# A hybrid decoder layer: the first norm's inverse root, GpSimd's early scaling, the first weight loads and two heads' key copies rearranged

## The chip, the core and the metric

The kernel runs on one core of a Trainium2 chip. The core has TensorE for matmuls (PE in the profile), VectorE (DVE), ScalarE (ACT), GpSimd (POOL) and SyncE (SP), which issues most DMAs. Each engine takes its instructions in order and waits on semaphores for the others. The metric is the device time of one execution in microseconds (us). A lower time is better.

## The reference

One decoder layer for a sequence of 1024 tokens and 1024 features, all in float32:

```python
u = rms_norm(x, g1);  aq, ak, av, hq, hf, hi, hg = split(u @ w_in)
attn = rms_norm(dilated_attention(aq, ak, av), g_a)      # 8 heads of 64
rec  = rms_norm(hgrn2(hq, hf, hi), g_h) * silu(hg)       # 4 heads of 128
h = x + concat(attn, rec) @ w_out
u = rms_norm(h, g2);  gate, val = split(u @ w_up)
h = h + (gelu(causal_conv3(gate)) * val) @ w_down
out = rms_norm(h, gf)      # rms_norm(x, g) = x * rsqrt(mean(x*x) + 1e-6) * g
```

## The kernel before

Data lie with features on the 128 partitions and tokens along a row. The sequence is worked in two halves of 512 tokens, called 0 and 1. Each float32 product is made from three matmuls on a pair of a rounded high part and a low remainder (`hi*hi`, `hi*lo`, `lo*hi`), so each operand is split first: a high copy and a subtraction. A `Ring` does it for the weights: it loads 128x512 pieces into `raww` by a DMA on SP's queue (L66), makes `whi` on ScalarE (L86) and `wlo` on VectorE or GpSimd (L88). Two pieces of head 1 go to buffers called `thw` and `tlw`.

The part that the change touches is the start, the first 62 us or so.

- **Load and split of x.** Eight chunks per half come in by SP (L389). `scale_x` makes `uhi` on ScalarE (L396) and `ulo` on VectorE (L397). `square_x` and `sum_x` collect the sum of squares. All these, and the first weights, are pinned in the order in which the code is written.
- **First products.** TensorE first runs some products of ones (`busy`, L380), then the combined query and key projections of heads 0 and 1, chunk by chunk (L459 to L462): two chunks of head 0, then the first two of head 1, and from there in turns.
- **The norm of x.** `rms1(hf)` sums the squares over partitions with a matmul and calls `rstd` twice: for `R1` (128x512) and for `R1T` (128x4, the same values with tokens on partitions). `rstd` takes Ln and Exp on ScalarE and sharpens the result with one Newton step of four VectorE operations (L319 to L322). `R1` scales `x` of a head (L548), `R1T` scales the values `v` (L566, L567).
- **A head's queries and keys** (`evac` in `qk_half`): `x = ps * R1` on VectorE, `qs` and one key copy on ScalarE (L549, L550), the second key copy, the low part of `qs` and `kl` on VectorE (L551, L552, L554). The zero halves of the two `kl` buffers are set by GpSimd at the start (L535).
- **Scores and values.** `score_steps(h, j)` makes the scores S (L584, L585) and P of two blocks of 128 queries: VectorE adds the mask and takes the row extreme (L587, and a 128x1 combination L591 where a row has two pieces), ScalarE takes Exp (L592), VectorE the reciprocal (L593), GpSimd multiplies (L596). `value_steps` transposes P on TensorE (L611 to L618) and multiplies by the values. The scores of (head 0, pair j+1) run beside the value steps of pair j, with other products filled in between.

TensorE's order is written out by hand. Where instructions of the other engines aren't pinned, a scheduler places them by its own costs. So a changed operation can shift the places of its neighbours. One DMA of `vec`, a table of gains and biases, is issued by ScalarE at the very start (L216). GpSimd then multiplies some of its columns by constants (L448), which are used much later.

Of the kernel before, what the change touches and what calls it, by code (L numbers as in the profile page):

```python
# [13 lines left out]
AF = mybir.ActivationFunctionType  # L14
ALU = mybir.AluOpType
PSUM = bass.MemoryType.PSUM

P = 128
SEQ = 1024
DM = 1024  # L20
# [6 lines left out]
EPS = 1e-6  # L27
# [6 lines left out]
V_AG = 8  # L34
V_HG = 12
V_LB = 16
V_G2 = 24
V_CW = 32
V_CB = V_CW + 3 * NFF
V_GF = V_CB + NFF  # L40
# [3 lines left out]
def f32(ap):  # L44
    return ap.bitcast(F32)


class Ring:


    def __init__(self, nc, pool, plan, tag="w", raws=5, depth=5, low=None):
        self.nc, self.pool, self.tag = nc, pool, tag
        self.RAWS, self.DEPTH, self.low = raws, depth, low or nc.gpsimd
        self.plan, self.at, self.live, self.n = list(plan), 0, {}, 0
        self.raws = 0
        self.aside = {}
        self.on_vector = ()
        self.order = self.pin = lambda ins: ins
        self.high = nc.scalar.copy

    def raw(self, src=None):
        t = self.pool.tile([P, H2], F32, tag=f"raw{self.tag}", name=f"raw{self.tag}{self.raws}", bufs=self.RAWS)
        self.raws += 1
        if src is not None:
            t = t[:, : src.shape[-1]]
            self.order(self.nc.sync.dma_start(t, src))  # L66
        return t

    def fill(self, count=99):
        while count and self.at < len(self.plan):  # L70
            key, src = self.plan[self.at]
            other = key in self.aside
            if (other and self.aside[key] is None) or (not other and self.n == self.DEPTH):
                return
            count -= 1
            i = self.at
            self.at += 1
            raw = src(self) if callable(src) else self.raw(src)
            w = raw.shape[-1]
            if other:  # L80
                hi, lo = self.aside[key](i)
            else:
                self.n += 1
                hi = self.pool.tile([P, H2], F32R, tag=f"{self.tag}hi", name=f"{self.tag}hi{i}", bufs=self.DEPTH)
                lo = self.pool.tile([P, H2], F32R, tag=f"{self.tag}lo", name=f"{self.tag}lo{i}", bufs=self.DEPTH)
            self.pin(self.high(hi[:, :w], raw))  # L86
            low = self.nc.vector if key in self.on_vector or key[0] in self.on_vector else self.low
            self.pin(low.tensor_sub(lo[:, :w], raw, f32(hi[:, :w])))  # L88
            self.live[key] = (hi, lo)
# [113 lines left out]
def hybrid_kernel(ctx: ExitStack, tc: tile.TileContext, xT, w_qk, w_tok, w_hg, w_out, w_up,  # L203
                  w_down, vecs, amask, hmask, out):
    nc = tc.nc
    PE, DVE, ACT, POOL = nc.tensor, nc.vector, nc.scalar, nc.gpsimd
    ctx.enter_context(tc.manual_schedule(engines={mybir.EngineType.PE}))

    def pool(name, side, **kw):
        return tc.tile_pool(name=name, bufs=1, side=side, reuse_waits="tile", **kw)  # L210
# [4 lines left out]
    vec = cpool.tile([P, V_N], F32, name="vec")  # L215
# [5 lines left out]
    lb = cpool.tile([P, 96], F32, name="lb")  # L221
    epool = ctx.enter_context(pool("eps", "right"))
    eps_ = epool.tile([P, 120], F32, name="eps")
    epst = eps_[:, 0:1]
    rv_cm = pool("rv", "right")
    rv = rv_cm.__enter__()
    ident = rv.tile([P, P], F32, name="ident")
    R1T = rv.tile([P, P], F32, name="R1T")
    DVE.memset(ones, 1.0)
    DVE.memset(eps_, EPS)  # L230
    make_identity(nc, ident)

    halves = [slice(0, H2), slice(H2, SEQ)]
# [75 lines left out]
    ring = Ring(nc, ringp, plan)  # L309
# [2 lines left out]
    def col(j):  # L312
        return vec[:, j : j + 1]

    def rstd(y, ms, t, ss, inv):

        ACT.activation(t, ss, AF.Ln, bias=epst, scale=inv)
        ACT.activation(y, t, AF.Exp, scale=-0.5)
        DVE.tensor_scalar(ms, ss, inv, EPS, op0=ALU.mult, op1=ALU.add)  # L319
        DVE.tensor_mul(t, y, y)  # L320
        DVE.scalar_tensor_tensor(ms, t, -0.5, ms, op0=ALU.mult, op1=ALU.mult)
        DVE.scalar_tensor_tensor(y, ms, 1.5, y, op0=ALU.add, op1=ALU.mult)  # L322
        return y

    def rstd_part(y, t, ss, inv):
# [20 lines left out]
    def rtile(name, dt=F32):  # L346
        return rv.tile([P, H2], dt, tag="r", name=name, bufs=8)
# [8 lines left out]
    R1 = up_.tile([P, SEQ], F32, name="R1")  # L356
# [4 lines left out]
    def bank(tag, name):  # L361
        return ps1.tile([P, H2], F32, tag=tag, name=name, bufs=2)
# [22 lines left out]
    pin = tc.keep_in_program_order  # L385
    xts = {hf: vtile([P, NCT, H2], F32, f"xt{hf}") for hf in range(2)}

    def load_x(hf, c):
        pin(nc.sync.dma_start(xts[hf][:, c], xT[c, :, halves[hf]]))  # L389
# [3 lines left out]
    def scale_x(hf, c):  # L393
        t = halves[hf]
        x = xts[hf][:, c]
        pin(ACT.mul(uhi[:, c, t], x, col(V_G1 + c)))  # L396
        pin(DVE.scalar_tensor_tensor(ulo[:, c, t], x, col(V_G1 + c), f32(uhi[:, c, t]), op0=ALU.mult, op1=ALU.subtract))  # L397
# [12 lines left out]
    def rms1(hf):  # L410
        ss = bank("t", f"ss{hf}")
        PE.matmul(ss, ones, sums[hf], start=True, stop=True)
        st = bank("t", f"sst{hf}")
        for i in range(4):
            PE.matmul(st[:, i : i + 1], sums[hf][:, i * P : (i + 1) * P], ones[:, 0:1], start=True, stop=True)
        rstd(R1[:, halves[hf]], rtile(f"ms{hf}"), rtile(f"rt{hf}"), ss, 1.0 / DM)
        tm = rv.tile([P, 64], F32, name=f"rst{hf}")
        rstd(R1T[:, 4 * hf : 4 * hf + 4], tm[:, 0:4], tm[:, 4:8], st[:, 0:4], 1.0 / DM)


    ring.order = ring.pin = pin
    load_x(0, 0)
    ring.high = DVE.tensor_copy
    ring.fill(1)
# [2 lines left out]
    load_x(0, 1)  # L427
    scale_x(0, 1)
    ring.fill(1)
    for c in (2, 3):  # L430
        load_x(0, c)
        scale_x(0, c)
# [11 lines left out]
            square_x(0, 4 + c, pin)  # L444
            sum_x(0, 4 + c, pin)
    ring.order = ring.pin = lambda ins: ins
    for v, n, inv in ((V_AG, 4, 1.0 / 512), (V_HG, 4, 1.0 / P), (V_G2, 8, 1.0 / DM), (V_GF, 8, 1.0 / DM)):
        POOL.tensor_scalar(vec[:, v : v + n], vec[:, v : v + n], -0.5 * inv, 0.0, op0=ALU.mult, op1=ALU.add)  # L448


    def dense(key, hf, evac, last, tag="mm"):

        t = halves[hf]
        ps = bank(tag, f"p{key}{hf}".translate({ord(x): "_" for x in "(', )"}))
        for c in range(NCT):
            hi, lo = ring.get((key, c // 4))
            s = slice((c % 4) * P, (c % 4 + 1) * P)
            b = between.get((key, hf, c), (0, 0))
            PE.matmul(ps, hi[:, s], uhi[:, c, t], start=(c == 0), stop=False)  # L459
            busy(b[0])  # L460
            PE.matmul(ps, hi[:, s], ulo[:, c, t], start=False, stop=False)
            PE.matmul(ps, lo[:, s], uhi[:, c, t], start=False, stop=(c == NCT - 1))  # L462
            busy(b[1])
            if last and c % 4 == 3:
                ring.done((key, c // 4))
            yield 0.65
        evac(ps)
# [60 lines left out]
    if True:  # L528
# [4 lines left out]
        for i in range(NQ):  # L533
            kl = at.tile([P, SEQ], F32R, name=f"kl{i}")
            POOL.memset(f32(kl[64:128]), 0.0)  # L535
            kls.append(kl)
        qk = {}

        def qk_half(h, hf, last, tag="mm"):
            t = halves[hf]  # L540

            def evac(ps):
                if hf == 0:
                    qk[h] = (at.tile([P, SEQ], F32R, tag="qs", name=f"qs{h}", bufs=NQ),
                             at.tile([P, SEQ], F32R, tag="kh", name=f"kh{h}", bufs=NQ), kls[h % NQ])
                qs, kh, kl = qk[h]
                x = at.tile([P, H2], F32, tag="x", name=f"x{h}_{hf}")
                DVE.tensor_mul(x, ps, R1[:, t])  # L548
                ACT.mul(qs[0:64, t], x[0:64], DH ** -0.5)  # L549
                ACT.copy(kh[64:128, t], x[64:128])  # L550
                DVE.tensor_copy(kh[0:64, t], x[64:128])  # L551
                DVE.scalar_tensor_tensor(qs[64:128, t], x[0:64], DH ** -0.5, f32(qs[0:64, t]),  # L552
                                         op0=ALU.mult, op1=ALU.subtract)
                DVE.tensor_sub(kl[0:64, t], x[64:128], f32(kh[64:128, t]))  # L554
            return dense(("qk", h), hf, evac, last, tag)
# [115 lines left out]
        for c in range(NCT):  # L671
            for g in pairs[1]:
                next(g)
            if c == 2:
                rms1(0)
                for g in pairs[0]:
                    next(g, None)
                ring.fill()
# [10 lines left out]
        fill.add(v0[3])  # L689
        fill.run()  # L690
        rms1(1)
        for c in range(4):
            for hf in range(2):
# [62 lines left out]
    with pool("hg", "right") as hg:  # L756
# [75 lines left out]
        tm = hg.tile([P, NG], F32, name="lb_m")  # L832
# [406 lines left out]
    with pool("ps2", "left", space=PSUM) as ps2:  # L1239
# [159 lines left out]
        for x, y in STAGES:  # L1399
# [27 lines left out]
            for d in range(KS):  # L1427
                src = ps[d]
# [3 lines left out]
                elif x == "s2":  # L1432
                    DVE.tensor_add(X[d], ps[d], X[d])
                    src = X[d]
# [83 lines left out]
```

## Time and profile before

| what | us |
|---|---|
| median of 3 runs | 1211.65 |
| lowest and highest | 1210.78 and 1213.84 |
| the profiled execution's own time | 1211.85 |
| its span in the trace | 1209.9 |
| PE busy in the span | 1193.9 (99%) |
| DVE busy | 951.6 (79%) |
| ACT busy | 627.2 (52%) |
| POOL busy | 299.2 (25%) |

The span runs from the first to the last traced instruction. 1.95 us of the execution's time lie around it. Busy shares are averages over stages with different limits. What a change at one place is worth is read at that place: which wait ends last there.

### The profile page before, as it was taken

The numbers are of one execution on the slowest core, as the hardware profiler recorded it, in microseconds if no ns is written. First come the engines' busy times: TensorE is split into PE (matmuls) and PEld (weight loads), VectorE is DVE, ScalarE is ACT, GpSimd is POOL, SyncE is SP. The second block draws the span as 40 slices with busy tenths as digits, with TensorE's granted clock in tenths as the row PEclk, the third lists the DMA queues.
The fourth block names the chain that finished last, engine by engine and source line by source line (L and its number), as shares of the span: only waits on it lengthen the run. The fifth ranks groups of instructions, "written<-read, shape, count | busy, mean of one in ns | idle before, by whom it ended". The sixth has DMA issues, their size and how long they took to land.

```text
span 1209.9 us, 17468 instructions
## 1 busy us (share of the span) xinstructions
PE 1193.9 (99%) x6014; PEld 1006.8 (83%) x6014; DVE 951.6 (79%) x1792; ACT 627.2 (52%) x1205; POOL 299.2 (25%) x278
## 2 busy tenths in 40 slices
PE   9999999999999999999999999999999999999996
PEld 7988888888888888888888888888888888888886
DVE  8867776666778776484999889898798878957986
ACT  8566667667656655454643343433434444444553
POOL 1254446545001014413221322312223100000000
PEclk9999999999999999999999999999999999999998
DMA  7021112123111123442023322333223267435532
GB/s 257 25 70 54 53 53 80 61 62 115 53 36 53 53 62 113 124 137 96 35 71 114 109 86 101 122 114 109 83 97 122 96 209 252 150 99 156 171 100 92
DMA packets 71817, 122.39 MB, mean 101 GB/s; under 512 B 7344, under 2 KB 17840, under 8 KB 71728
## 3 DMA queue, kind: packets, MB, share of 16 engines
q1 hardware_dynamic: 60928, 101.80, 26.8%
q10 hardware_dynamic: 10800, 19.47, 4.2%
q8 instruction: 47, 0.77, 0.3%
q14 instruction: 42, 0.34, 0.1%
HBM read 97.65 MB, written 23.59 MB: 100 GB/s over the span
## 4 chain that ended last, share of the span: by engine, by line
PE 93%; issue 2%; DVE 2%; ACT 1%; POOL 0%; DMA 0%; SPq 0%; DVEq 0%; ACTq 0%; POOLq 0%
PE p L1125 10%; PE p L1123 10%; PE p L1124 10%; PE ds L1418 3%; PE ds L1417 3%; PE ds L1416 3%; PE po L1027 2%; PE po L1029 2%; PE po L1028 2%; PE da L1418 2%; PE da L1417 2%; PE da L1416 2%; PE S L584 1%; PE piv L513 1%; PE S L585 1%
## 5 line engine op out<-in xcount | busy, mean ns | idle before, releaser
L88 POOL TENSOR_TENSOR wlo<-raww,whi 128x512 fp32r<-128x512 f32 x141 | 207.5, 1482 | 383.5 <-ACT whi L86 274.1
L86 ACT CAST whi<-raww 128x512 fp32r<-128x512 f32 x276 | 168.3, 618 | 190.6 <-DVE raww L120 64.8
L88 DVE TENSOR_TENSOR wlo<-raww,whi 128x512 fp32r<-128x512 f32 x136 | 97.4, 716 | 22.6 <-ACT whi L86 22.5
L86 ACT CAST whi<-r 128x512 fp32r<-128x512 f32 x70 | 43.6, 622 | 83.6 <-PE ds L1417 51.4
L596 POOL TENSOR_SCALAR P<-P,st 128x512 f32<-128x512 f32 (+2 forms) x96 | 56.3, 596 | 110.8 <-DVE st L593 62.2
L587 DVE CUSTOM_DVE_ANT_0 P<-S,mask 128x512 f32<-128x512 f32 (+2 forms) x96 | 52.1, 553 | 29.9 <-PE S L585 29.0
L592 ACT ACTIVATE P<-P,st 128x128 f32<-128x128 f32 (+3 forms) x64 | 49.7, 776 | 32.9 <-DVE st L587 16.6
L623 DVE TENSOR_TENSOR tl<-T,th 128x512 fp32r<-128x512 f32 (+1 forms) x80 | 50.7, 634 | 16.6 <-ACT th L622 15.6
L88 DVE TENSOR_TENSOR wlo<-r,whi 128x512 fp32r<-128x512 f32 x70 | 47.9, 686 | 20.2 <-ACT whi L86 20.1
L1418 PE MATMUL ds<-fhi,wlo 128*128 128x512 f32 x160 | 62.3, 389 | 0.0
L1417 PE MATMUL ds<-flo,whi 128*128 128x512 f32 x160 | 62.3, 389 | 0.0
L1416 PE MATMUL ds<-fhi,whi 128*128 128x512 f32 x160 | 62.2, 389 | 0.0
L1123 PE MATMUL p<-b1h,whi 128*128 128x512 f32 x160 | 62.2, 389 | 0.0
L1124 PE MATMUL p<-b1l,whi 128*128 128x512 f32 x160 | 62.2, 389 | 0.0
L1125 PE MATMUL p<-b1h,wlo 128*128 128x512 f32 x160 | 62.2, 389 | 0.0
L1145 DVE SCALAR_TENSOR_TENSOR cv<-g,vec,cv 128x511 f32<-128x511 f32 (+2 forms) x92 | 56.1, 615 | 4.7 <-ACT cv L1142 3.7
L1390 POOL TENSOR_TENSOR facc<-facc,sqf 128x256 f32<-128x256 f32 x4 | 2.9, 732 | 223.1 <-ACT sqf L1389 223.1
L1152 ACT ACTIVATE cv<-cv 128x512 f32<-128x512 f32 x44 | 27.8, 633 | 55.6 <-DVE cv L1145 55.5
L622 ACT CAST th<-T 128x512 fp32r<-128x512 f32 (+1 forms) x80 | 42.9, 536 | 23.5 <-PE T L615 20.9
L86 ACT CAST fhi<-rawf 128x512 fp32r<-128x512 f32 x70 | 43.1, 616 | 15.2 <-DMA rawf<-spT 6.5
L88 DVE TENSOR_TENSOR flo<-rawf,fhi 128x512 fp32r<-128x512 f32 x70 | 47.9, 684 | 4.0 <-ACT fhi L86 4.0
L1416 PE MATMUL da<-fhi,whi 128*128 128x512 f32 x120 | 46.7, 389 | 0.0
(670 smaller groups left out, 3833.5 us busy)
## 6 DMA issues: line engine op xcount, KB each, us to landing
raww<-in_w_up_dram SPq DMA_DIRECT2D x88, 256.0 KB, 3.1
raww<-in_w_tok_dram SPq DMA_DIRECT2D x52, 256.0 KB, 2.6
rawf<-spT SPq DMA_DIRECT2D x40, 256.0 KB, 2.7
r<-in_w_down_dram SPq DMA_DIRECT2D x40, 256.0 KB, 3.4
raww<-in_w_hg_dram SPq DMA_DIRECT2D x32, 256.0 KB, 2.6
raww<-in_w_out_dram SPq DMA_DIRECT2D x32, 256.0 KB, 2.6
spB<-a ACTq DMA_DIRECT2D x30, 256.0 KB, 2.3
spT<-t ACTq DMA_DIRECT2D x30, 256.0 KB, 2.0
```

What stands on the lines that cost most here:

```text
L86: self.pin(self.high(hi[:, :w], raw))
L88: self.pin(low.tensor_sub(lo[:, :w], raw, f32(hi[:, :w])))
L587: DVE.tensor_tensor_reduce(Pt[:, k0 : k0 + w], S[:, :w], mask[:, m : m + w], -1.0, BIG * 3, op0=ALU.add, op1=ALU.min, accum_out=st[:, k0 / ...
L596: POOL.tensor_scalar(e, e, st[:, 3:4], 1.0, op0=ALU.mult, op1=ALU.mult)
L623: DVE.tensor_sub(tl[:, :n], T[:, :n], f32(th[:, :n]))
L1123: PE.matmul(ps, hi[:, s], bhi, start=(start and n == 0), stop=False)
L1124: PE.matmul(ps, hi[:, s], blo, start=False, stop=False)
L1125: PE.matmul(ps, lo[:, s], bhi, start=False, stop=(stop and n == len(rhs) - 1))
L1145: DVE.scalar_tensor_tensor(dst, x, col(V_CW + j * NFF + f), dst, op0=ALU.mult, op1=ALU.add)
L1416: PE.matmul(ps[d], hi[:, s], ahi, start=(k == 0), stop=False)
L1417: PE.matmul(ps[d], hi[:, s], alo, start=False, stop=False)
L1418: PE.matmul(ps[d], lo[:, s], ahi, start=False, stop=(k == NPAIR - 1))
```

## The change

Five edits, all in the first stage.

1. `rstd` no longer makes the mean `ms` first. Exp's result is squared on ScalarE, VectorE multiplies it by the sum plus a constant (one operation), ScalarE applies `1.5 - 0.5*inv*t` (Identity with a bias from a column of `eps`), and VectorE multiplies by Exp's result. So each call has two VectorE operations where there were four, and two more on ScalarE. `rstd` is called four times: `R1` and `R1T`, each for both halves.
2. The constant tile `eps` gets 1.5 in its upper columns, by a second memset.
3. GpSimd's scaling of `vec` moves behind the memsets of `kl`, and is pinned there.
4. The DMAs of the first two weight pieces go out on ScalarE's queue instead of SP's.
5. For heads 0 and 1 the second key copy is made by ScalarE, not by VectorE (four instructions, one per head and half).

```diff
--- before.py
+++ after.py
@@ -57,13 +57,14 @@
         self.on_vector = ()
         self.order = self.pin = lambda ins: ins
         self.high = nc.scalar.copy
+        self.queue = nc.sync
 
     def raw(self, src=None):
         t = self.pool.tile([P, H2], F32, tag=f"raw{self.tag}", name=f"raw{self.tag}{self.raws}", bufs=self.RAWS)
         self.raws += 1
         if src is not None:
             t = t[:, : src.shape[-1]]
-            self.order(self.nc.sync.dma_start(t, src))
+            self.order(self.queue.dma_start(t, src))
         return t
 
     def fill(self, count=99):
@@ -221,13 +222,14 @@
     lb = cpool.tile([P, 96], F32, name="lb")
     epool = ctx.enter_context(pool("eps", "right"))
     eps_ = epool.tile([P, 120], F32, name="eps")
-    epst = eps_[:, 0:1]
+    epst, onehalf = eps_[:, 0:1], eps_[:, 64:65]
     rv_cm = pool("rv", "right")
     rv = rv_cm.__enter__()
     ident = rv.tile([P, P], F32, name="ident")
     R1T = rv.tile([P, P], F32, name="R1T")
     DVE.memset(ones, 1.0)
-    DVE.memset(eps_, EPS)
+    DVE.memset(eps_[:, 0:64], EPS)
+    DVE.memset(eps_[:, 64:120], 1.5)
     make_identity(nc, ident)
 
     halves = [slice(0, H2), slice(H2, SEQ)]
@@ -312,14 +314,14 @@
     def col(j):
         return vec[:, j : j + 1]
 
-    def rstd(y, ms, t, ss, inv):
+    def rstd(y, t, ss, inv):
 
         ACT.activation(t, ss, AF.Ln, bias=epst, scale=inv)
         ACT.activation(y, t, AF.Exp, scale=-0.5)
-        DVE.tensor_scalar(ms, ss, inv, EPS, op0=ALU.mult, op1=ALU.add)
-        DVE.tensor_mul(t, y, y)
-        DVE.scalar_tensor_tensor(ms, t, -0.5, ms, op0=ALU.mult, op1=ALU.mult)
-        DVE.scalar_tensor_tensor(y, ms, 1.5, y, op0=ALU.add, op1=ALU.mult)
+        ACT.activation(t, y, AF.Square)
+        DVE.scalar_tensor_tensor(t, ss, EPS / inv, t, op0=ALU.add, op1=ALU.mult)
+        ACT.activation(t, t, AF.Identity, bias=onehalf, scale=-0.5 * inv)
+        DVE.tensor_mul(y, t, y)
         return y
 
     def rstd_part(y, t, ss, inv):
@@ -413,12 +415,13 @@
         st = bank("t", f"sst{hf}")
         for i in range(4):
             PE.matmul(st[:, i : i + 1], sums[hf][:, i * P : (i + 1) * P], ones[:, 0:1], start=True, stop=True)
-        rstd(R1[:, halves[hf]], rtile(f"ms{hf}"), rtile(f"rt{hf}"), ss, 1.0 / DM)
+        rstd(R1[:, halves[hf]], rtile(f"rt{hf}"), ss, 1.0 / DM)
         tm = rv.tile([P, 64], F32, name=f"rst{hf}")
-        rstd(R1T[:, 4 * hf : 4 * hf + 4], tm[:, 0:4], tm[:, 4:8], st[:, 0:4], 1.0 / DM)
+        rstd(R1T[:, 4 * hf : 4 * hf + 4], tm[:, 0:4], st[:, 0:4], 1.0 / DM)
 
 
     ring.order = ring.pin = pin
+    ring.queue = nc.scalar
     load_x(0, 0)
     ring.high = DVE.tensor_copy
     ring.fill(1)
@@ -427,6 +430,7 @@
     load_x(0, 1)
     scale_x(0, 1)
     ring.fill(1)
+    ring.queue = nc.sync
     for c in (2, 3):
         load_x(0, c)
         scale_x(0, c)
@@ -444,8 +448,6 @@
             square_x(0, 4 + c, pin)
             sum_x(0, 4 + c, pin)
     ring.order = ring.pin = lambda ins: ins
-    for v, n, inv in ((V_AG, 4, 1.0 / 512), (V_HG, 4, 1.0 / P), (V_G2, 8, 1.0 / DM), (V_GF, 8, 1.0 / DM)):
-        POOL.tensor_scalar(vec[:, v : v + n], vec[:, v : v + n], -0.5 * inv, 0.0, op0=ALU.mult, op1=ALU.add)
 
 
     def dense(key, hf, evac, last, tag="mm"):
@@ -534,6 +536,8 @@
             kl = at.tile([P, SEQ], F32R, name=f"kl{i}")
             POOL.memset(f32(kl[64:128]), 0.0)
             kls.append(kl)
+        for v, n, inv in ((V_AG, 4, 1.0 / 512), (V_HG, 4, 1.0 / P), (V_G2, 8, 1.0 / DM), (V_GF, 8, 1.0 / DM)):
+            pin(POOL.tensor_scalar(vec[:, v : v + n], vec[:, v : v + n], -0.5 * inv, 0.0, op0=ALU.mult, op1=ALU.add))
         qk = {}
 
         def qk_half(h, hf, last, tag="mm"):
@@ -548,7 +552,7 @@
                 DVE.tensor_mul(x, ps, R1[:, t])
                 ACT.mul(qs[0:64, t], x[0:64], DH ** -0.5)
                 ACT.copy(kh[64:128, t], x[64:128])
-                DVE.tensor_copy(kh[0:64, t], x[64:128])
+                (ACT.copy if h < 2 else DVE.tensor_copy)(kh[0:64, t], x[64:128])
                 DVE.scalar_tensor_tensor(qs[64:128, t], x[0:64], DH ** -0.5, f32(qs[0:64, t]),
                                          op0=ALU.mult, op1=ALU.subtract)
                 DVE.tensor_sub(kl[0:64, t], x[64:128], f32(kh[64:128, t]))
```

The scheduler moves other instructions with these. At the start of ScalarE's queue, `raww0` and `raww1` are the first pieces of the weights of heads 0 and 1, and `uhi` the first chunks of x. Before:

```order
L216 DMA vec_63<-in_vecs_dram 128x128
L217 ACT_TABLE_LOAD
L396 ACTIVATE uhi_86<-xt0_104,vec_63 128x512 x2
L86 CAST thw1_120<-raww1_118 128x512
L396 ACTIVATE uhi_86<-xt0_104,vec_63 128x512 x2
L86 CAST whi2_132<-raww2_130 128x512
L86 CAST thw3_138<-raww3_136 128x512
```

After:

```order
L217 DMA vec_63<-in_vecs_dram 128x128
L218 ACT_TABLE_LOAD
L67 DMA raww0_108<-in_w_qk_dram 128x512
L398 ACTIVATE uhi_87<-xt0_105,vec_63 128x512 x2
L67 DMA raww1_119<-in_w_qk_dram 128x512
L87 CAST thw1_121<-raww1_119 128x512
L398 ACTIVATE uhi_87<-xt0_105,vec_63 128x512 x2
L87 CAST whi2_133<-raww2_131 128x512
L87 CAST thw3_139<-raww3_137 128x512
```

The second weight load now stands behind two activations that wait for chunks of x, and `thw1`, which needs that load, right behind it. On SP's queue at the start, before (`mask` is the attention mask, 512 KB, `xt` the chunks of x, `raww4` the first value weights):

```order
L389 DMA xt0_104<-in_xT_dram 128x512
L66 DMA raww0_107<-in_w_qk_dram 128x512
L389 DMA xt0_104<-in_xT_dram 128x512
L66 DMA raww1_118<-in_w_qk_dram 128x512
L389 DMA xt0_104<-in_xT_dram 128x512 x2
L66 DMA raww2_130<-in_w_qk_dram 128x512
L66 DMA raww3_136<-in_w_qk_dram 128x512
L389 DMA xt0_104<-in_xT_dram 128x512 x4
L389 DMA xt1_105<-in_xT_dram 128x512 x8
L530 DMA mask_205<-in_amask_dram 128x1024
L66 DMA raww4_328<-in_w_tok_dram 128x512
```

After:

```order
L391 DMA xt0_105<-in_xT_dram 128x512 x4
L532 DMA mask_202<-in_amask_dram 128x1024
L67 DMA raww2_131<-in_w_qk_dram 128x512
L67 DMA raww3_137<-in_w_qk_dram 128x512
L391 DMA xt0_105<-in_xT_dram 128x512 x4
L391 DMA xt1_106<-in_xT_dram 128x512 x8
L67 DMA raww4_328<-in_w_tok_dram 128x512
```

Besides the two weight loads that left, the mask has moved ahead of the second weight pieces and of chunks 4 to 7 of x. On VectorE around the norm of half 1 (`rt1`, `rst1` and `ms1` are its temporaries, `x0_1` is head 0's projection of half 1, `P0_2` and `P0_3` are blocks of its scores), before:

```order
L322 SCALAR_TENSOR_TENSOR R1_88<-ms1_545,R1_88 128x512
L322 SCALAR_TENSOR_TENSOR R1T_76<-rst1_553,R1T_76 128x4
L587 ISA P0_2_595,st0_2_596<-S0_2_0_597,mask_205 128x384
L587 ISA st0_2_596 128x1
L548 TENSOR_TENSOR x0_1_632<-p__qk___0_1_268,R1_88 128x512
L567 SCALAR_TENSOR_TENSOR v0_436<-pV0_4_568,R1T_76,v0_436 128x4x64
L593 RECIPROCAL st0_2_596<-st0_2_596 128x1
L587 ISA P0_3_614,st0_3_615<-S0_3_0_616,mask_205 128x512
L587 ISA st0_3_615 128x1
L551 CAST kh0_311<-x0_1_632 64x512
L552 SCALAR_TENSOR_TENSOR qs0_310<-x0_1_632,qs0_310 64x512
L593 RECIPROCAL st0_3_615<-st0_3_615 128x1
```

After:

```order
L591 ISA P0_2_594,st0_2_595<-S0_2_0_596,mask_202 128x384
L591 ISA st0_2_595 128x1
L324 TENSOR_TENSOR R1_89<-rt1_545,R1_89 128x512
L324 TENSOR_TENSOR R1T_76<-rst1_552,R1T_76 128x4
L552 TENSOR_TENSOR x0_1_631<-p__qk___0_1_269,R1_89 128x512
L571 SCALAR_TENSOR_TENSOR v0_436<-pV0_4_567,R1T_76,v0_436 128x4x64
L597 RECIPROCAL st0_2_595<-st0_2_595 128x1
L591 ISA P0_3_613,st0_3_614<-S0_3_0_615,mask_202 128x512
L591 ISA st0_3_614 128x1
L556 SCALAR_TENSOR_TENSOR qs0_310<-x0_1_631,qs0_310 64x512
L558 TENSOR_TENSOR kl0_204<-x0_1_631,kh0_311 64x512
L552 TENSOR_TENSOR x1_1_680<-p__qk___1_1_273,R1_89 128x512
```

`R1` is now finished behind the mask addition of `P0_2`, not ahead of it. The key copy is gone, and `x1_1` has moved ahead of the reciprocal of `P0_3`. TensorE's own order is the same instruction by instruction.

## Rows read from the trace of the kernel before

**Rows 1.** The page: busy us and share; granted clock by 40 slices, in tenths.

```profile
PE 1193.9 (99%) x6014; PEld 1006.8 (83%) x6014; DVE 951.6 (79%) x1792; ACT 627.2 (52%) x1205; POOL 299.2 (25%) x278
...
PEclk9999999999999999999999999999999999999998
```

**Rows 2.** TensorE's waits: us in total, times, longest.

```profile
PE T L612 <- POOL P L596: 2.6, 1, 2.6
```

**Rows 3.** Stretches around that wait: length, busy us (count) by engine, granted clock.

```profile
56.00:63.40 7.40, 4.69 (x35) 4.17 (x34) 6.45 (x18) 5.17 (x11) 4.23 (x6) 1.00 0.10 35
63.40:66.80 3.40, 3.40 (x15) 3.01 (x14) 1.56 (x5) 1.65 (x4) 2.26 (x4) 0.50 0.22 77
```

**Rows 4.** Timeline of the first 9.5 us: start, length, engine, line.

```profile
1.16 1.28 ACT L217 ACT_TABLE_LOAD   x1 [1.16 <-PEq L1506]
1.19 0.44 SPq L66 DMA_DIRECT2D raww<-in_w_qk_dram  x1
...
2.15 0.43 SPq L66 DMA_DIRECT2D raww<-in_w_qk_dram  x1
...
4.29 0.95 POOL L535 MEMSET kl<- 64x1024 f32 x1
4.38 1.13 DVE L86 CAST whi<-raww 128x512 fp32r<-128x512 f32 x1 [3.25 <-DMA raww<-in_w_qk_dram]
...
5.66 0.47 PE L459 MATMUL p__qk___0_0_211<-uhi,whi 128*128 128x512 f32 x1 [0.83 <-DVE whi L86]
...
6.18 0.72 ACT L396 ACTIVATE uhi<-xt,vec 128x512 fp32r<-128x512 f32 x1 [1.65 <-DMA xt<-in_xT_dram]
...
7.59 0.62 ACT L86 CAST thw<-raww 128x512 fp32r<-128x512 f32 x1 [0.69 <-DMA raww<-in_w_qk_dram]
...
8.24 0.69 DVE L88 TENSOR_TENSOR tlw<-raww,thw 128x512 fp32r<-128x512 f32 x1 [0.55 <-ACT thw L86]
...
9.36 0.40 PE L462 MATMUL p__qk___1_0_225<-uhi,tlw 128*128 128x512 f32 x1
```

**Rows 5.** Timeline ahead of the first scores.

```profile
38.47 0.48 DVE L567 SCALAR_TENSOR_TENSOR v<-pV,R1T,v 128x256 fp32r<-128x256 f32 x1
...
39.78 0.22 PE L584 MATMUL S<-kh,qs 128*128 128x128 f32 x1
```

**Rows 6.** Timeline behind the norm of half 1.

```profile
48.28 0.56 DVE L587 CUSTOM_DVE_ANT_0 P<-S,mask 128x384 f32<-128x384 f32 x1 [0.29 <-PE S L585]
...
48.77 0.69 DVE L548 TENSOR_TENSOR x<-p__qk___0_1_268,R 128x512 f32<-128x512 f32 x1
...
50.79 0.73 ACT L592 ACTIVATE P<-P,st 128x512 f32<-128x512 f32 x1
...
51.98 1.19 POOL L596 TENSOR_SCALAR P<-P,st 128x512 f32<-128x512 f32 x1 [1.38 <-DVE st L593]
...
53.58 0.27 PE L612 MATMUL T<-ident,P 128*128 128x128 f32 x1
```

**Rows 7.** ScalarE by line, first 70 us: count, busy us, mean ns.

```profile
L550 ACT CAST kh<-x 64x512 fp32r<-64x512 f32 x4 | 2.5, 618 | 0.1
...
L317 ACT ACTIVATE rt<-ss,eps 128x512 f32<-128x512 f32 x2 | 1.4, 687 | 0.6 <-PE ss L412 0.6
```

**Rows 8.** VectorE by line, first 70 us.

```profile
L551 DVE CAST kh<-x 64x512 fp32r<-64x512 f32 x4 | 1.7, 422 | 0.1
```

**Rows 9.** Timeline around TensorE's longest wait.

```profile
58.42 0.62 ACT L86 CAST whi<-raww 128x512 fp32r<-128x512 f32 x1
...
59.12 1.28 POOL L88 TENSOR_TENSOR wlo<-raww,whi 128x512 fp32r<-128x512 f32 x1 [0.45 <-ACT whi L86]
...
59.29 1.13 DVE L591 TENSOR_TENSOR st<-st 128x1 f32<-128x1 f32 x1
...
60.51 0.94 ACT L592 ACTIVATE P<-P,st 128x768 f32<-128x768 f32 x1 [1.47 <-DVE st L591]
...
61.92 1.14 POOL L596 TENSOR_SCALAR P<-P,st 128x512 f32<-128x512 f32 x2 [1.52 <-DVE st L593]
...
62.66 0.33 PE L612 MATMUL T<-ident,P 128*128 128x128 f32 x1 [2.63 <-POOL P L596]
```

## The prediction

> **What bounds the kernel now.** I read the page's first part, then TensorE's waits, then the timeline at the two places that the waits name. TensorE is busy in 1193.9 of 1209.9 us [rows 1], so the end moves only with TensorE's stream: with what makes it start late, wait, or run at its lower clock. The waits show one of size: 2.6 us for a GpSimd multiplication of P [rows 2]. It costs more than itself. Around it the granted clock is 1.00, and in the 3.40 us from 63.4 it is 0.50, the lower of the two levels (1.2 and 2.4 GHz), with TensorE busy throughout [rows 3]. Half of 3.40 is 1.70 us lost. So 2.63 + 1.70 = 4.33 us lie there. The rest within reach is the start: the first product waits 0.83 us for a weight piece's high copy on VectorE [rows 4]. Other stages keep their instructions in their order, and I give them nothing.
>
> How the wait at 60 us comes about is read backwards [rows 9]. The transpose at 62.66 needs P of block 5, scaled by GpSimd from 61.92. That needs Exp, which started at 60.51, when VectorE's tiny combination L591 was done. L591 has 128x1 elements and took 1.13 us: it started at 59.29, while GpSimd's `wlo` subtraction ran from 59.12 to 60.40, and ended with it. TensorE stood from about 59.9.
>
> **The change part by part.** Durations are from the one profiled execution; its own time is 1211.85 us, 0.20 above the median shown.
>
> *GpSimd's scaling behind its zeros.* The first high copy took 1.13 us from 4.38, during a `kl` memset from 4.29 to 5.24; a VectorE copy of as many columns takes 0.42 [rows 4, 8]. After the change the memset follows `ident` at once and is over before 4. The copy then saves 1.13 - 0.42 = 0.71 us, if the weight lands as early as before. The scaling is used much later and costs nothing.
>
> *First weights by ScalarE's queue.* Before, SP issued them at 1.19 and 2.15, and they were first used at 4.38 and 7.59: 3.19 and 5.44 us later [rows 4]. Now the first stands behind the table load that starts at 1.16. If the queue passes the load, the issue is at about 1.2, as before; if it waits for it, at 2.44, and the first product comes 1.25 - 0.71 = 0.5 later. No row shows a DMA behind a table load. I take the first, and the second is inside the bounds below. The second stands behind two activations, the later of which waits for chunk 1 of x. That chunk was used at 6.18 [rows 4]. With a weight less ahead of it in SP's queue it lands between the 4.38 at which the transfer ahead of it was used and 6.18. I take 5.2. Then the piece is used at 5.2 + 3.2 = 8.4; bounds 4.4 + 3.2 = 7.6 and 6.2 + 5.4 = 11.6. The chain behind it is copy 0.65 with its hop and subtraction 0.69; the product that needs `tlw` ran at 9.36 though `tlw` was done at 8.93 [rows 4], a slack of 0.43. So TensorE's start moves by (8.4 - 7.59) - 0.43 = **+0.4 us**, bounds -0.4 (limited by the copy's gain) and +3.6. Queued behind the late copy on ScalarE are chunks 2 and 3 of x and the second weight halves, and on SP 512 KB of mask now go ahead of those halves. No row gives their landing. I take it that they stay just ahead, and count the copy's 0.71 us at nothing for it.
>
> The Trainium skill, "DMA: Bandwidth & Descriptors", section "Issuing engines are not separate DMA queues", speaks against this edit: transfers from any queue run on the same 16 engines and interleave, and a second issuer saves only the issue time. By it the second weight shares the engines with the mask and x that SP has queued. Taken at the 5.44 us that this piece took before behind others, it would be used at 10.65 and the sum come to 1212.1. No run here shows two queues at work on long transfers at once.
>
> *The root.* In half 0 it is hidden. Its products are `qs`, `kl` and `v`, first wanted by the scores at 39.78; VectorE's last piece ahead of them starts at 38.47 and ends at 38.95, 0.8 us early [rows 5]. The new chain passes twice to ScalarE and stands behind a weight copy (0.62) more, but VectorE is rid there of two 512-column operations (1.4) and two key copies (0.8). I take 0; if the cover goes, the scores are some 0.5 late.
>
> In half 1 the new chain after Exp is Square 0.62 (as a copy), VectorE 0.69, Identity 0.69 (as Ln with its bias) [rows 4, 7], 2.0 us, against three VectorE operations of 0.69. The last multiplication no longer fits ahead of the mask addition at 48.28 (it waits for the scores). So it starts at 48.78, and head 0's `x` at 49.5 instead of 48.77: +0.7 [rows 6]. ScalarE then makes `qs` and two key copies instead of one, 0.62 each with a hop between, from 50.2 to 52.15, and starts Exp of block 3 there instead of at 50.79: +1.36. GpSimd's multiplication moves with it from 51.98 to 53.35, or 53.5 with `x` of head 1 now ahead of the reciprocal. It took 1.19 there; in rows 9 TensorE goes 0.74 after such a start, and I take 0.74. TensorE wants the block at 53.58 [rows 6], and gets it at 54.25: a new wait of about **0.65 us**, bounds 0 and 1.5.
>
> *The key copies.* VectorE loses 2 x 0.42 in half 1, ScalarE gains 2 x 0.62 [rows 7, 8]. VectorE's 0.73 us of lateness is then paid back: its combination L591 of block 5 comes at 59.29 + 0.73 - 0.84 = 59.2. ScalarE's weight copy, which stood at 58.42 [rows 9], is late by 0.65 at least (TensorE, whose products free its buffer, is late by that) and by 1.24 at most. I take 0.85: it ends at 59.9, and `wlo` on GpSimd starts at 59.95. L591 is now ahead of it and isn't held. Exp of block 5 starts behind the weight copy at 59.9 (before 60.51) and its reciprocal is done by 61.2. GpSimd is free at 59.95 + 1.28 = 61.23, and the transpose goes 0.74 after that, at 62.0 instead of 62.66 [rows 9]: **-0.65 us** on TensorE's stream, bounds -2.6 (no wait) and +0.45 (rival B). Since TensorE arrives 0.65 late, its wait there is 62.0 - 59.9 - 0.65 = 1.45.
>
> *The clock.* Waits of 0.65 and 1.45 us, with products between them, stand for one of 2.63. The drop to 0.50 follows only that long wait [rows 3]; the slice with the 0.83 us at the start reads 9, as all but the last do [rows 1]. 1.45 is nearer to 0.83 than to 2.63, so I take the clock to stay: **-1.70 us**. Bounds 0 and -1.70.
>
> *Sum.* 0.4 - 0.65 - 1.7 = -1.95, so 1211.85 - 1.95 = **1209.9 us**.
>
> **The rivals.**
>
> A. The whole wait goes. If the second weight lands early and ScalarE's and GpSimd's steps come half a microsecond sooner than I place them, both waits vanish. That is -4.33 from the wait and clock, with the start anywhere from -0.4 to +0.4: 1211.85 - 4.33 = 1207.5. For it: VectorE's removed work. Against it: ScalarE, not VectorE, is now late for blocks 3 and 5. Chance 0.2.
>
> B. Slower: L591 is held again. It precedes `wlo` by 0.75 us in my working. If VectorE is that much later, or ScalarE earlier at its weight copy, L591 stands behind `wlo` until 61.2, Exp runs to 62.2, and GpSimd's multiplication goes from 62.4, the transpose from 63.1: +0.45 on 62.66. TensorE then waits 0.65 and 2.6, the clock falls as before, and the start adds 0.4: 1211.85 + 0.85 = 1212.7. It decides where L591 and the weight copy's end change places. Chance 0.2. The Trainium skill, "SBUF — State Buffer", section "Who interferes with whom", has it as a rule: of a VectorE operation with two SBUF inputs and a GpSimd operation that reads SBUF, the one that comes first blocks the other fully. The 1.13 us of L591 agree.
>
> C. The change doesn't do what it says: it shortens VectorE's list but TensorE's two waits together still bring the clock down. Then 0.4 - 0.65 + 0 = -0.25, 1211.6. Chance 0.15.
>
> The late bound of the weights (+3.6) can come on top of any of them; half of it on the forecast would give 1211.4, on B 1214.
>
> **How the numbers follow.** The forecast has 0.45, its own range is 1208.6 to 1211.4. For 8 in 10 the range takes in A and most of B with a late weight: 1207.0 to 1213.6. 0.3% of 1211.65 is 3.6 us, about what a measurement of this kernel can tell from no change: faster means below 1208.0, slower above 1215.3. Faster comes from most of A and a little of the forecast, 0.17. Slower needs B and the late bound together, 0.06. The rest, 0.77, is no change.
>
> **What would show it.** In the changed kernel's waits, the 2.6 us for GpSimd's P should be gone and two shorter ones stand in its place, near 53.6 and 60 to 62. The granted clock should be 1.00 from the start to the last slice. The first high copy should take about 0.4 us. `thw` should be cast at about 8.4 with an idle ahead of it put down to its DMA. L591 near 59 should be short, with `wlo` starting behind it. I am wrong if `thw` comes before 8 or after 9.5, if the clock falls near 63 all the same, or if no wait for P is left.

## The result and the profile after

| | before | after |
|---|---|---|
| median, us | 1211.32 (22 runs) | 1213.74 (22 runs) |
| ratio after/before, 95% interval | | 1.0021 [1.0016, 1.0027] |
| profiled execution, us | 1211.85 | 1213.03 |
| its span, us | 1209.9 | 1211.1 |

The changed kernel is slower by 0.21%, some 2.4 us. Forecast was 1209.9, 1.8 us less than before. The median also lies above 1213.6, the end of the range that I gave 8 in 10. A few executions, such as one of the changed kernel (5600.26 us) and one of e11 (1707.74), ran far longer than all others of their kernel, and the ratios leave them out. The two profiled executions differ by 1.2 only: that of before lies 0.5 above its kernel's median, that of after 0.7 below.

The waits of TensorE after (total, times, longest):

```profile
PE p__qk___0_0_212 L461 <- ACT uhi L398: 1.8, 1, 1.8
PE T L616 <- POOL P L600: 1.7, 2, 1.1
PE S L588 <- DVE st L591: 1.1, 2, 0.7
...
PE p__qk___1_0_226 L461 <- ACT thw L87: 0.6, 1, 0.6
```

The 2.6 us of [rows 2] are gone, and two shorter waits for P stand in their place. The first and the last line are new: they lie at the start. The timeline of after, first 12 us, then the sum of the norm of half 1 and a transpose at 70 us:

```profile
1.17 1.28 ACT L218 ACT_TABLE_LOAD   x1 [1.17 <-PEq L1510]
1.20 0.43 ACTq L67 DMA_DIRECT2D raww<-in_w_qk_dram  x1
...
2.59 0.43 SPq L532 DMA_DIRECT2D mask<-in_amask_dram  x1
...
3.85 0.89 SPq L67 DMA_DIRECT2D raww<-in_w_qk_dram  x2
...
5.83 0.72 ACT L398 ACTIVATE uhi<-xt,vec 128x512 fp32r<-128x512 f32 x1 [1.26 <-DMA xt<-in_xT_dram]
5.84 0.35 ACTq L67 DMA_DIRECT2D raww<-in_w_qk_dram  x1
6.08 0.43 DVE L87 CAST whi<-raww 128x512 fp32r<-128x512 f32 x1 [4.95 <-DMA raww<-in_w_qk_dram]
...
6.66 0.76 PE L461 MATMUL p__qk___0_0_212<-uhi,whi 128*128 128x512 f32 x1 [1.82 <-ACT uhi L398]
...
11.22 0.62 ACT L87 CAST thw<-raww 128x512 fp32r<-128x512 f32 x1 [4.66 <-DMA raww<-in_w_qk_dram]
...
11.89 0.50 PE L461 MATMUL p__qk___1_0_226<-uhi,thw 128*128 128x512 f32 x1 [0.60 <-ACT thw L87]
...
46.48 1.02 PE L414 MATMUL ss<-sq,ones 128*128 128x512 f32 x2
...
70.30 0.27 PE L615 MATMUL T<-ident,P 128*128 128x128 f32 x1
```

The same two instructions before:

```profile
43.12 1.02 PE L412 MATMUL ss<-sq,ones 128*128 128x512 f32 x2
...
69.39 0.27 PE L611 MATMUL T<-ident,P 128*128 128x128 f32 x1
```

TensorE runs the same instructions in the same order in both, so the distance between equal rows is the time lost so far. At the sum it is 46.48 - 43.12 = 3.36 us, at the transpose 70.30 - 69.39 = 0.91. So the start cost 3.36, and the stretch up to 70 us gave 2.45 back. The second weight piece went out at 5.84 and was used at 11.22, where [rows 4] have 2.15 and 7.59. The first came 1.7 us later than before (6.08 for 4.38); its `whi`, which the first product needs besides the `uhi` named above, was done at 6.51. The first product ran 0.76 us instead of 0.47. The cast is 0.43 long, as forecast.

The middle, after:

```profile
57.79 0.33 PE L616 MATMUL T<-ident,P 128*128 128x128 f32 x1 [0.60 <-POOL P L600]
...
62.36 0.15 DVE L595 TENSOR_TENSOR st<-st 128x1 f32<-128x1 f32 x1
...
63.08 1.29 POOL L89 TENSOR_TENSOR wlo<-raww,whi 128x512 fp32r<-128x512 f32 x1 [0.83 <-ACT whi L87]
...
64.34 1.14 POOL L600 TENSOR_SCALAR P<-P,st 128x512 f32<-128x512 f32 x2
...
65.09 0.33 PE L616 MATMUL T<-ident,P 128*128 128x128 f32 x1 [1.14 <-POOL P L600]
```

The two transposes answer to those at 53.58 and 62.66 in [rows 6, 9]: they are 4.21 and 2.43 us later in the span, where the sum was 3.36 later. The combination (now L595) took 0.15 us instead of 1.13, since it started ahead of `wlo`. The granted clock from 62 to 70 us is 1.00 (the last number but two), where [rows 3] had 0.50:

```profile
62.00:70.00 8.00, 6.86 (x52) 6.37 (x51) 5.50 (x18) 6.74 (x13) 6.44 (x9) 1.00 0.22 66
```

### The profile page after: what moved, and what is told of

It is laid out like the page before. It is cut to its first block, busy times and chain, and to the rows that moved or that the text cites. A ratio compares the mean times of both kernels' runs of the same rounds, so it can differ in the third digit from the quotient of the medians.

```text
span 1211.1 us, 17476 instructions
## 1 busy us (share of the span) xinstructions
PE 1194.2 (99%) x6014; PEld 1006.6 (83%) x6014; DVE 946.3 (78%) x1781; ACT 631.8 (52%) x1217; POOL 298.5 (25%) x278
## 4 chain that ended last, share of the span: by engine, by line
PE 93%; issue 2%; DVE 2%; ACT 1%; DMA 1%; POOL 0%; DVEq 0%; SPq 0%; ACTq 0%; POOLq 0%
PE p L1129 10%; PE p L1128 10%; PE p L1127 10%; PE ds L1422 3%; PE ds L1420 3%; PE ds L1421 3%; PE po L1031 2%; PE po L1033 2%; PE po L1032 2%; PE da L1422 2%; PE da L1420 2%; PE da L1421 2%; PE piv L515 1%; PE S L588 1%; PE piv L517 1%
```

## The experiments

Ratios are to the kernel before, run on the same chip, with 95% intervals.

| run | median, us | ratio |
|---|---|---|
| e1_weights_sync | 1209.88 | 0.9988 [0.9979, 0.9997] |
| e2_queue_only | 1216.74 | 1.0042 [1.0030, 1.0055] |
| e3_root_copies | 1209.96 | 0.9986 [0.9977, 0.9995] |
| e5_mask_behind | 1213.41 | 1.0017 [1.0008, 1.0026] |
| e6_first_only | 1212.15 | 1.0003 [0.9994, 1.0012] |
| e7_both_early | 1212.24 | 1.0005 [0.9996, 1.0014] |
| e8_more_warm | 1213.64 | 1.0021 [1.0012, 1.0030] |
| e9_root_only | 1214.16 | 1.0027 [1.0018, 1.0036] |
| e10_copies_only | 1209.92 | 0.9990 [0.9981, 0.9999] |
| e11_copies_wlo | 1208.40 | 0.9973 [0.9963, 0.9984] |
| e12_plus_gpsimd | 1208.10 | 0.9971 [0.9958, 0.9984] |
| e13_copies_wlo_again | 1208.31 | 0.9969 [0.9958, 0.9981] |

### Which edit costs: e1, e2, e3

e1, from the changed kernel:

```diff
-    ring.queue = nc.scalar
```

> The changed kernel with the first two weight loads back on SP's queue, in their old places; its four other edits stay. Theory Q (the queue edit alone costs the 3.4 us by which the norm's sum is late at 46.5 us): thw is cast near 7.6 again, the sum comes at 42.5 to 43.1, and the time is 1213.7 - 3.4 = 1210.3, or 1209.6 if the 0.7 us of the short first cast counts too. Rival M (what is lost lies in the middle, in the root and the key copies, and the late start is made good by slack behind it): the time stays within 0.5 of the changed kernel's 1213.7.

e2, the kernel before with `ring.queue` as in the change.

> The kernel before with the queue edit alone. Theory Q: thw near 11.2, the norm's sum 3 to 3.4 us later than the 43.1 of the kernel before, time 1211.3 + 3.4 = 1214.7. Rival M: 1211.3 to 1211.8, since the products of the start have slack behind them. It also shows whether the mask's place ahead of the second weight halves comes from the queue edit (Q) or from another one.

e3, the kernel before with the change's `rstd` and its key copies (`(ACT.copy if h < 2 else DVE.tensor_copy)`).

> The kernel before with the new root and the two heads' key copies on ScalarE, and nothing else. Theory Q: the wait of 2.6 us for GpSimd's P falls into two of 0.6 and 1.1, no granted clock of 0.50 near 63; time 1211.3 - 0.9 = 1210.4, and 1208.7 if the 1.7 us of the low clock are in the usual run too. Rival M: 1211.3 or more, up to 1213.7.

Without the queue edit the changed kernel takes 1209.88, 3.9 us less. With that edit alone the kernel before takes 1216.74, 5.4 us more. Theory Q (the queue edit costs the time) holds and rival M (the middle costs it) falls. In e1 the sum and the transpose come at:

```profile
43.28 1.02 PE L414 MATMUL ss<-sq,ones 128*128 128x512 f32 x2
...
67.08 0.27 PE L614 MATMUL T<-ident,P 128*128 128x128 f32 x1
```

That is +0.16 and -2.31 against before: the middle alone gave 2.47. The sum came 0.2 us later than Q had it. e3 agrees (1209.96). e2 lost 2.0 us more than Q said: its sum came at 47.05, 3.93 late, and behind the wait of 2.6 us, which it shares with the kernel before, the low clock lasts 6.80 us instead of 3.40:

```profile
65.70:72.50 6.80, 5.92 (x24) 5.54 (x25) 3.48 (x11) 3.32 (x7) 4.89 (x7) 0.50 0.18 70
```

Its mask load has moved ahead too, so that came from the queue edit.

### What of the queue edit costs: e5, e6, e7, e8

e5, from the changed kernel, the mask's load moved to the end of the pinned loads:

```diff
+    mask = at.tile([P, SEQ], F32, name="mask")
+    pin(nc.sync.dma_start(mask, amask))
     ring.order = ring.pin = lambda ins: ins
```

> The changed kernel, with the mask's load pinned behind all chunks of x on SP's queue (it had moved ahead of the second weight halves and chunks 4 to 7 of x). Rival K (the mask's 512 KB are what delays the weight on ScalarE's queue and what follows): the second weight lands 1.4 to 2 us earlier than 11.2, and the time falls to 1211.7 to 1212.3. Theory Q in its narrow form (the weight is late since it is issued at 5.84 behind two activations and shares the engines with x): thw still after 9.5 and the time 1213.0 to 1213.7.

e6, as e5, and `ring.queue = nc.sync` ahead of `scale_x(0, 0)`:

```diff
     ring.high = ACT.copy
+    ring.queue = nc.sync
     scale_x(0, 0)
```

> The changed kernel with only the first weight piece on ScalarE's queue; the second goes out by SP behind two chunks of x, and the mask's load is pinned behind all x. Theory Q (the landing of the second piece sets the loss; it was late since it went out at 5.84 behind two activations and landed behind what SP had issued till then): thw is cast near 7 to 7.5, the norm's sum comes 1.5 to 2.5 earlier than 46.5, and the time is 1213.7 - 2 = 1211.7, within 0.7. Rival C (the late first product and the lower clock up to 9.7 us set the loss): first product still after 6.5, clock rise still near 9.7, and the time at 1213 or more.

e7, from the changed kernel:

```diff
     ring.fill(1)
+    key, src = ring.plan[1]
+    second = ring.raw(src)
+    ring.plan[1] = key, lambda r: second
     ring.high = ACT.copy
```

> The changed kernel with both weight loads issued on ScalarE's queue at the start, the second right behind the first and ahead of the activations. Theory Q: the second is issued near 1.65 instead of 5.84, lands by 7.5, and the time falls by about 2, to 1211.7. A plain sharing rival (two queues take turns, whatever the place of issue): the first piece still lands at 6 to 6.5 and the second near it, at about 6.5 to 7, time 1211 to 1212. Rival C: 1213 or more.

e8, from the changed kernel:

```diff
-    busy(8)
+    busy(14)
```

> The changed kernel with 14 instead of 8 products of ones ahead of the first real product, so that TensorE doesn't stand between 4.83 and 6.66. Rival C (the lower clock up to 9.7 us costs the time): granted clock 1.00 from about 5.4 on, the norm's sum about 1.5 to 2 earlier, time near 1212. Theory Q: the clock is high early, but the products then wait longer for thw at 11.2 (1.5 to 2.5 us instead of 0.6), the sum comes where it came and the time stays at 1213.2 to 1213.9.

Rival C's lower clock shows in the length of the products: in the changed kernel the one at 6.66 took 0.76 us, the one at 9.89 took 0.48. In e8 the first took 0.47. Yet the time stays (1213.64), and what TensorE gains at the start it waits for `thw`, so e8 rejects rival C for the changed kernel:

```profile
PE p__qk___1_0_232 L461 <- ACT thw L87: 1.7, 1, 1.7
...
11.58 0.62 ACT L87 CAST thw<-raww 128x512 fp32r<-128x512 f32 x1 [4.47 <-DMA raww<-in_w_qk_dram]
...
46.84 1.02 PE L414 MATMUL ss<-sq,ones 128*128 128x512 f32 x2
```

The sum comes 46.84 - 11.58 = 35.26 us behind the cast of `thw`. It is 35.26 in the changed kernel too (46.48 - 11.22) and in e5 (below), 35.28 in e2 (47.05 - 11.77) and 35.24 in e1 (43.28 - 8.04), though the first product and the clock at the start differ among these runs. So the landing of the second piece sets the sum in all five.

e5 rejects the mask: 1213.41. The second piece was as late without it:

```profile
6.47 0.35 ACTq L67 DMA_DIRECT2D raww<-in_w_qk_dram  x1
...
11.97 0.62 ACT L87 CAST thw<-raww 128x512 fp32r<-128x512 f32 x1 [4.78 <-DMA raww<-in_w_qk_dram]
...
47.23 1.02 PE L414 MATMUL ss<-sq,ones 128*128 128x512 f32 x2
```

From issue to use it took 11.97 - 6.47 = 5.50 us; with the mask in front, in the changed kernel, 5.38. The DMA engines are full in either case: their busy share from 4.0 to 9.7 us is 1.02 in the changed kernel and 0.96 in e5.

What the piece waits for is in the changed kernel's trace. By 5.84 SP had issued four chunks of x, the mask and two weight pieces, 2.10 MB. The rows give packets, MB and the share of the engines' time, q1 for SP's queue up to 6.0 us and from there to 9.0, then q10 for ScalarE's queue from 9.0 to 11.2:

```profile
q1 hardware_dynamic: 429, 0.80, 50.4%
...
q1 hardware_dynamic: 529, 1.23, 104.1%
...
q10 hardware_dynamic: 144, 0.26, 31.0%
```

From 6.0 to 9.0 ScalarE's queue moved nothing. The 0.26 MB of the second piece came only when SP's queue had moved 2.03 of its 2.10 MB. So this load ran behind nearly all that was issued ahead of it, though on another queue.

In e6, where SP issues the second piece at 1.65, the sum is 0.37 us later than before, and the median is 1212.15, 1.3 less than in e5, from which e6 differs by this load alone:

```profile
7.18 0.62 ACT L87 CAST thw<-raww 128x512 fp32r<-128x512 f32 x1 [1.22 <-DMA raww<-in_w_qk_dram]
...
43.49 1.02 PE L414 MATMUL ss<-sq,ones 128*128 128x512 f32 x2
```

In e7, where ScalarE issues it right behind the first, `thw` is cast at 8.01:

```profile
1.22 0.90 ACTq L67 DMA_DIRECT2D raww<-in_w_qk_dram  x2
...
6.82 0.43 DVE L87 CAST whi<-raww 128x512 fp32r<-128x512 f32 x1 [5.68 <-DMA raww<-in_w_qk_dram]
...
7.39 0.47 PE L464 MATMUL p__qk___0_0_212<-uhi,whi 128*128 128x512 f32 x1 [2.57 <-ACT uhi L398]
...
8.01 0.62 ACT L87 CAST thw<-raww 128x512 fp32r<-128x512 f32 x1 [0.64 <-DMA raww<-in_w_qk_dram]
```

So an early issue on ScalarE's queue is worth 1.5 us by the medians (1212.24). By the ratios e6 and e7 are still about 1.8 and 2.1 us behind SP's queue (e1). Two queues at once delay the first piece: used 5.6 us after its issue in e7, 4.88 in the changed kernel, 3.19 on SP's queue [rows 4]. In e7's profiled execution what rival C names then does set the loss: its sum came at 46.22, TensorE stood 2.57 us, and its granted clock (the last number but two) was 0.50 behind that:

```profile
8.09:11.50 3.41, 3.41 (x16) 3.12 (x15) 3.41 (x6) 3.41 (x7) 0.00 (x0) 0.50 1.09 405
```

The Trainium skill, "DMA: Bandwidth & Descriptors", section "Issuing engines are not separate DMA queues", says that transfers from any engine share the same 16 engines and interleave. e7 agrees: the two loads were used 5.6 and 6.3 us after their issue. The second load of the changed kernel does not: it had no packet between 6.0 and 9.0 us, while SP's queue ran.

The profiled execution of e7 took 1213.50 us, 1.3 above its kernel's median, and that of e6 1209.87, 2.3 below. So neither trace shows a usual execution of its kernel, and what keeps the medians of e6 and e7 behind e1 stays open.

### Root against copies: e9, e10

e9, the kernel before with the change's `rstd` alone (and the 1.5 in `eps` that it needs).

> The kernel before with the new root alone; both key copies stay as they were (one on VectorE). By the prediction's working VectorE is then late by 0.73 at the combination of block 5, which stands behind wlo again: a wait of 2.6 us or more for GpSimd's P remains, the clock falls, and the time is 1211.3 to 1212.2. Rival (the root by itself is what removes the wait, the copies do nothing): no wait over 1.5, time 1210.0 like the run with both.

e10, the kernel before with the key copies alone:

```diff
-                DVE.tensor_copy(kh[0:64, t], x[64:128])
+                (ACT.copy if h < 2 else DVE.tensor_copy)(kh[0:64, t], x[64:128])
```

> The kernel before with the two heads' key copies on ScalarE and nothing else. If the copies repay what the root delays (the prediction's step, and the run with the root alone at 1214.2), then without the root VectorE's combination of block 5 comes 0.84 us earlier than before, ahead of wlo; GpSimd multiplies P from about 60.0 and the transpose goes near 60.7: one wait of 0.9 us or less and none for block 3, granted clock 1.00, time 0.5 to 1.5 below the run with root and copies (1210.0), so 1208.5 to 1209.5. Rival (root and copies only work together, or ScalarE's extra 0.62 us make Exp late by themselves): two waits as with both, or one of 2.6, and 1210 to 1211.5.

By the medians the root alone costs 2.6 us (1214.16) and the copies alone gain 1.9 (1209.92; 1.2 by the ratio). In e9 the combination is held by `wlo` once more, as the prediction's step had it. But the wait is longer still, and the time 2 us above the 1211.3 to 1212.2 that I expected:

```profile
59.76 1.28 POOL L88 TENSOR_TENSOR wlo<-raww,whi 128x512 fp32r<-128x512 f32 x1 [0.44 <-ACT whi L86]
...
59.92 1.13 DVE L592 TENSOR_TENSOR st<-st 128x1 f32<-128x1 f32 x1
...
62.76 1.26 POOL L88 TENSOR_TENSOR wlo<-raww,whi 128x512 fp32r<-128x512 f32 x1 [1.72 <-ACT whi L86]
...
64.00 1.15 POOL L597 TENSOR_SCALAR P<-P,st 128x512 f32<-128x512 f32 x2
...
64.75 0.33 PE L613 MATMUL T<-ident,P 128*128 128x128 f32 x1 [4.07 <-POOL P L597]
```

A second `wlo` now stands ahead of P on GpSimd. In e10 I was wrong about the wait, one of 2.25 us is left, and by 0.4 us about the time (1208.5 to 1209.5 expected):

```profile
59.24 0.15 DVE L593 RECIPROCAL st<-st 128x1 f32<-128x1 f32 x1
...
59.71 1.26 POOL L88 TENSOR_TENSOR wlo<-raww,whi 128x512 fp32r<-128x512 f32 x1 [1.98 <-ACT whi L86]
...
60.96 1.15 POOL L596 TENSOR_SCALAR P<-P,st 128x512 f32<-128x512 f32 x2
...
61.70 0.33 PE L612 MATMUL T<-ident,P 128*128 128x128 f32 x1 [2.25 <-POOL P L596]
```

The reciprocal was done at 59.39, but P started at 60.96, since `wlo` stands ahead of it in GpSimd's order and itself waited for `whi`. VectorE isn't the bound any more: GpSimd's order is. The wait is only 0.38 us shorter than before, but no low clock follows it: the granted clock from 62 to 70 us is 1.00, where [rows 3] had 0.50. This trace is of an execution 0.8 below e10's median.

### The better kernel: e11, e12, e13

e11, e10 and one `wlo` piece on VectorE:

```diff
-        ring.on_vector += [(("out", 1, d), i) for d in range(NCT) for i in range(2)]
+        ring.on_vector += [(("out", 1, d), i) for d in range(NCT) for i in range(2)] + [("V1_0", 1)]
```

> As the run with the copies alone, and the low part wlo of the second piece of the first value weights of group 1 is made by VectorE instead of GpSimd, so that GpSimd has nothing but P between 57 and 62 us. If GpSimd's wlo still holds P back there, the time falls by up to 0.5 more; if Exp and the reciprocal are the last to come, it stays within 0.3 of the run with the copies alone, or rises by up to 0.7 as VectorE's 0.69 us go ahead of the combination of block 6.

e12, e11 with GpSimd's scaling behind its zeros, and e13, e11 again, beside it.

> As the run with the copies and VectorE's wlo (1208.4), and GpSimd's scaling of vec moved behind its zeros. If the first high copy's 1.13 us (held by the zeros in some executions, 0.43 in others) reaches the end, the time falls by 0.3 to 0.7, to 1207.7 to 1208.1; if its cover on TensorE takes it (the prediction counted nothing), it stays within 0.3 of the run beside it without this edit.

> The copies and VectorE's wlo once more, beside the run with the GpSimd edit, to be compared with it on one chip: 1208.4 within 0.4, ratio to the kernel before 0.9963 to 0.9984. If the earlier time was chance, nearer to the 1209.9 of the copies alone.

e11 takes 1208.40, 1.5 less than e10 by the medians (2.1 by the ratios) and 0.27% less than before. P starts soon behind its reciprocal:

```profile
59.64 0.15 DVE L593 RECIPROCAL st<-st 128x1 f32<-128x1 f32 x1
...
59.96 1.58 POOL L596 TENSOR_SCALAR P<-P,st 128x512 f32<-128x512 f32 x2 [1.83 <-DVE st L593]
...
60.71 0.33 PE L612 MATMUL T<-ident,P 128*128 128x128 f32 x1 [0.86 <-POOL P L596]
```

The gain is larger than the 0.5 expected, and e13 repeats it (1208.31). e12 lies 0.21 below e13, and the two intervals cover each other: the GpSimd edit can't be told from nothing, as the prediction counted it.

## Why the prediction failed, step by step

- **The start, +0.4: failed.** It measured +3.36 (46.48 against 43.12), just inside the bound of +3.6 that I gave it, and `thw` came at 11.22, past the 9.5 that I had named as a sign of being wrong. Two numbers in this term were wrong. I took the second load's issue at 5.2, and it was 5.84, since chunk 1 of x shared the engines with the first weight piece (up to 6.0 SP's queue moved 0.80 MB and ScalarE's 0.33). And I took 3.2 us from issue to use, the first piece's time with little ahead of it; it took 5.38, behind what SP had issued. The row for this very piece was there: 5.44 in [rows 4], which I used for the bound only. With 5.2 + 5.44 = 10.64 the start would have been +2.6 and the sum 1212.1, the figure that the prediction set aside beside the page's rule. e6 and the 35.2 to 35.3 us between `thw` and the sum in five runs show that the landing of the second piece sets the loss; e5 and e8 show that in the changed kernel neither the mask nor the lower clock does.
- **The first piece.** The issue passed the table load, as taken (1.20). That the two queues delay each other's pieces I did not price: 4.88 us instead of 3.19. e8 shows that this was hidden behind the second piece here.
- **The middle, -0.65 - 1.70 = -2.35: right in its steps.** It measured 0.91 - 3.36 = -2.45 in the changed kernel and -2.47 in e1. The new wait for block 3 was 0.60 (0.65 forecast), the wait for block 5 1.14 (1.45), the combination started 0.72 ahead of `wlo` (0.75), and the clock stayed. That the copies pay back what the root delays is shown by e9. The close sum is partly luck: up to block 5's transpose the stream gained 3.36 - 2.43 = 0.93 instead of 0.65, and behind it 2.43 - 0.91 = 1.52 instead of 1.70.
- **Two readings in the middle.** TensorE stood before block 5 from 62.66 - 2.63 = 60.03, not 59.9, so the forecast wait should have been 1.32. And that the slice with the 0.83 us reads 9 says nothing of the clock: the third slice, which holds the drop to 0.50, reads 9 too. The choice that 1.45 keeps the clock was a guess that held: no drop followed 1.14 in the changed kernel, nor 2.25 in e10.
- **Later stages, taken as nothing.** In e1 the 2.31 us gained at 70 us are 1.1 at the end of the span (1208.8 against 1209.9), about the 1.4 between the medians. The second wait near 617 us (last section) is part of it.
- **Rivals.** A (the whole wait goes) and B (the combination is held again) did not come; B's mechanism is what e9 shows, the root without the copies. C failed as well, since the clock stayed. The outcome is the one I left as an addition to any of them, the late weights, and I gave it no chance of its own: 1211.85 - 2.35 + 3.36 = 1212.9, against 1213.03 in the profiled execution. That it can end on the slow side was in the numbers I had.
- **What stays open.** Between 70 us and the end the profiled changed kernel loses another 0.3, of which one longer wait for scores (0.7 instead of 0.4) is a part that is read from the traces and was not tried. Of the 2.4 us between the medians, 1.2 are in the two traces; the rest is the place of each profiled execution among its kernel's runs. Why e6 and e7 stay behind e1 is not shown.

## What to carry to other kernels

Where a load moves to another queue, price it by its own time from issue to use behind all that is in flight, and by the place that it then has behind its new engine's instructions; a second queue gave it no lane of its own here, where the DMA engines were full. When a wait names an engine that is not busy, look at what stands ahead of the awaited instruction in that engine's order: a subtraction moved off GpSimd was worth about as much (1.5 us by the medians, 2.1 by the ratios) as the copies moved off VectorE (1.9 and 1.2).

## What the runs showed of the hardware

- The first high copy isn't always held by GpSimd's memset. In e11 it was (cast 1.13 us), in e13, the same kernel, it wasn't. There `vec` landed later, so that the memset began behind the cast:

```profile
4.31 0.95 POOL L535 MEMSET kl<- 64x1024 f32 x1
4.41 1.13 DVE L86 CAST whi<-raww 128x512 fp32r<-128x512 f32 x1 [3.28 <-DMA raww<-in_w_qk_dram]
```

```profile
4.24 0.43 DVE L86 CAST whi<-raww 128x512 fp32r<-128x512 f32 x1 [3.11 <-DMA raww<-in_w_qk_dram]
...
4.78 0.95 POOL L535 MEMSET kl<- 64x1024 f32 x1
```

- A low clock followed TensorE's waits of 2.63 us (before), 4.07 (e9), 2.62 (e2), and at the start 2.41 (e2), 2.57 (e7) and 2.63 (e5), and none followed 2.25 (e10), 1.14 (the changed kernel) and 0.86 (e11).
- Near 617 us the profiled e1, e2, e3 and e7 wait twice for `wlo` (1.1 to 1.2 us in all), and the other traces once (0.5), with the same instructions on TensorE. What decides between the two was not tried, nor whether it varies between executions of one kernel.
